# Where the adaLN columns and the context squares stand in the opening of a hybrid attention/GLA layer

## The chip, the cores and the metric

One NeuronCore of a Trainium2 chip runs the whole kernel. The metric is device time in microseconds of one execution, the median of several runs; lower is better.

## The reference, cut to what matters

One backbone layer over 256 latent tokens and 256 context tokens, width 2048. Both streams are normalized, scaled and shifted by columns that come from the conditioning vectors, and go through one wide projection. The change lies in this first part alone:

```python
mod_x = jnp.split((jax.nn.silu(c) @ w_mod[l] + b_mod[l])[:, None, :], 6, axis=-1)
mod_c = jnp.split((jax.nn.silu(c_ctx) @ w_mod[l] + b_mod[l])[None, None, :], 6, axis=-1)
# modulate(x, g, shift, scale) = rms_norm(x, g) * (1 + scale) + shift
... = proj(modulate(x, g_mix[l], mod_x[0], mod_x[1]))          # qa, ka, va, qb, kb, vb, ...
... = proj(modulate(ctx, g_mix[l], mod_c[0], mod_c[1]))
```

Windowed attention, gated linear attention, the merge and the convolutional feed-forward part follow; they are the same in both kernels.

## The kernel before

Activations lie transposed: channels on the 128 partitions, 256 tokens along the free axis, in 16 channel tiles ("kt") of 128. Every fp32 operand of a large product is split into a high part (ScalarE, `whi`, `h00hi`, line 207 or 495) and the rest (VectorE, `wlo`, `h00lo`, line 208 or 496), and three products are added up: high by high, high by low, low by high. In a tile's name h00lo the first digit is the stream (0 latent, 1 context), the second the half of the channels.

The scale and shift columns aren't there when the kernel starts. They are computed in five groups of channel tiles, `GROUPS` = (first tile, count) = (0,2), (2,2), (4,4), (8,4), (12,4), so that the projection can start on the first two tiles while the rest of the modulation matrix is still being loaded. For each group and each of the two parts (part 1 is the scale, part 0 the shift) `mod_both` makes steps: each step loads 1 MB of the matrix (`mraw`) and multiplies it by the conditioning vector (`pm`, line 95; 16 profile records of 256 columns for a step of the first two groups, 8 records of 512 columns for one of the others). After the last step VectorE transposes the result (`mtr`, line 324), and `end` turns it into columns: two small products on TensorE (`pcol`, line 95), four copies on VectorE (line 334) and an addition. `affine_scale` then multiplies the tokens by scale and by the row of 1/rms (`rrow`, lines 485 and 488), `affine_shift` adds the shift and splits (lines 495 and 496).

The row of 1/rms of the context comes from `square_sums(1)`: four squares on ScalarE (line 427, each 128x1024), additions on VectorE (lines 433 and 435), a sum over the channels on TensorE (`pr`, line 448), and the chain of `factor_row` (lines 457 to 462).

Order. Within the opening all TensorE instructions are chained in the order of the code (`pe_seq`), and all loads in theirs (`load`, queue of SyncE). On ScalarE and VectorE a scheduler sets the order, with single ties by `in_order(a, b)`. The projections used in the opening are columns QB (two blocks of 512), KB and VB of `w_in`. They accumulate in four PSUM banks (`acc`), which an evacuation has to free (line 503 into `qb0`, 556 and 572 into the tile kb0, 558 and 575 into vb0 for the first group, additions at line 505 for later ones).

The first group runs QB, QB+512, KB, VB for the latents, then KB, VB for the context. While the second group is multiplied, the steps of the third are called at six places, by `mid()`: before and inside QB+512, after QB+512, inside KB, after KB, inside VB. The list `steps` says how many steps each place takes. `end` of the third group was put off to the next `tick()` (the start of the next pair of channel tiles) by `defer(0, fn)`.

Of the kernel before, what the change touches and what calls it, by code (L numbers as in the profile page):

```python
# [11 lines left out]
AF = mybir.ActivationFunctionType  # L12
# [12 lines left out]
QA, KA, VA, QB, KB, VB, RB = 0, 2048, 2560, 3072, 4096, 5120, 7168  # L25
# [6 lines left out]
def layer_kernel(ctx, tc, A, out):  # L32
    nc = tc.nc
    V, S, G, PE = nc.vector, nc.scalar, nc.gpsimd, nc.tensor
# [12 lines left out]
    w_in = A["w_in"][0]  # L47
# [16 lines left out]
    def in_order(*ins):  # L64

        for a, b in zip(ins, ins[1:]):
            tc.add_manual_dep(b, a.name, mybir.DependencyInfo(
                mybir.DependencyClass.NoSync, mybir.DependencyReason.DATA), reason="order")
# [12 lines left out]
    def mm(*a, **k):  # L81

        r = pe_seq(PE.matmul(*a, **k))  # L83
        last[0] = r.ins
        return r
# [63 lines left out]
    def defer(n, fn):  # L149

        later.append([n, fn])
# [37 lines left out]
    def wload(src):  # L189
        n = src.shape[0] // P  # L190
        raw = wr.tile([P, 2, 512], F32, name="raw", tag="raw")
        load(raw[:, 0:n, :], src.rearrange("(c p) d -> p c d", p=P))
        return raw
# [65 lines left out]
    def proj_T(w, c0, kts, rhs, evac, mid=None):  # L259

        n = len(rhs)
        per = 2 // n
        banks = [acc.tile([P, 512], F32, name="acc", tag="acc") for _ in range(4 // per)]
        for k0 in kts[::2]:
            tick()
            nk = min(2, kts[-1] + 1 - k0)
            hi, lo = wsplit(w[k0 * P:(k0 + nk) * P, c0:c0 + 512])
            for part in range(2):
                if part:
                    (mid or midway)()  # L270
                for f in range(4):
                    for k in range(nk):
                        kt = k0 + k
                        w_ = (lo if part else hi)[:, k, f * P:(f + 1) * P]
                        for i, r in enumerate(rhs):
                            b = (f % per) if n == 1 else i
                            o = banks[f // per][:, b * T:(b + 1) * T]
                            ahi, alo = r(kt)
                            mm(o, w_, ahi, start=(kt == kts[0] and b == 0 and part == 0),
                                      stop=(kt == kts[-1] and part == 1), skip_group_check=True)  # L280
                            if part == 0:
                                mm(o, w_, alo, start=False, stop=False, skip_group_check=True)
        for i in range(len(banks)):
            evac(i, banks[i])
# [111 lines left out]
    def rms_scale(ss, n, shape):  # L396
# [13 lines left out]

    groups = GROUPS
    mods = [[mod_both(part, t0, n, dst, put) for part, dst in ((1, scale1), (0, shift1))]
            for (t0, n), put in zip(groups, [None, None] + 3 * [lambda fn: defer(0, fn)])]

    rrow1 = []
    kbt = M("kb0", [P, 4, 512])
# [2 lines left out]
    def square_sums(s):  # L419

        pr = bank("pr", (P, T), side=True)
        parts, whole = [], None
        for i in range(4):
            x_ = xr[2 * s + i // 2][:, (i % 2) * 4:(i % 2) * 4 + 4, :]
            q = wr.tile([P, 4, T], F32, name="sq", tag="raw")
            if s + i:
                S.activation(q, x_, AF.Square)
            else:
                V.tensor_tensor(q, x_, x_, op=ALU.mult)
                parts.extend(q[:, k, :] for k in range(4))  # L430
                continue
            h = q[:, 0:2, :]
            V.tensor_tensor(h, h, q[:, 2:4, :], op=ALU.add)
            if s and whole is not None:
                V.tensor_tensor(whole, whole, h, op=ALU.add)
            elif s:
                whole = h
            elif i == 2:
                V.tensor_tensor(h[:, 0, :], h[:, 0, :], h[:, 1, :], op=ALU.add)
                parts.append(h[:, 0, :])  # L440
            else:
                parts.extend(h[:, k, :] for k in range(2))
        if s:
            parts = [whole[:, 0, :], whole[:, 1, :]]

        def add_up(lo, hi):
            for i in range(lo, hi):
                pe_seq(PE.matmul(pr, ones[:, 0:P], parts[i], start=(i == 0), stop=(i == len(parts) - 1)))

        return pr, add_up  # L450
# [19 lines left out]
    def h_all(s):  # L470
        return lambda kt: (hh[s][kt // 8][:, kt % 8, :], hl[s][kt // 8][:, kt % 8, :])
# [11 lines left out]
    def affine_scale(s, t0, n):  # L483
        sc = scale1[:, s, t0:t0 + n]
        V.scalar_tensor_tensor(sc, sc, 1.0, gm1[:, t0:t0 + n], op0=ALU.add, op1=ALU.mult)
        for kt in range(t0, t0 + n):
            xk = xr[2 * s + kt // 8][:, kt % 8, :]
            V.scalar_tensor_tensor(xk, xk, scale1[:, s, kt:kt + 1], rrow1[s], op0=ALU.mult, op1=ALU.mult)

    def affine_shift(s, t0, n):  # L490
        for kt in range(t0, t0 + n):
            xk = xr[2 * s + kt // 8][:, kt % 8, :]
            sh = shift1[:, s, kt:kt + 1]
            hi, lo = hh[s][kt // 8][:, kt % 8, :], hl[s][kt // 8][:, kt % 8, :]
            j = S.activation(hi, xk, AF.Identity, bias=sh).ins
            i = V.scalar_tensor_tensor(lo, xk, sh, hi.bitcast(F32), op0=ALU.add, op1=ALU.subtract).ins
        return i, j


    def add_to(dst, first):  # L500
        def evac(i, b):
            if first:
                S.activation(dst(i), b, AF.Copy)
            else:
                V.tensor_tensor(dst(i), dst(i), b, op=ALU.add)
        return evac
# [35 lines left out]
    qb0 = [W2("fc", "qb0", [P, 512]) for _ in range(4)]  # L542
    kts = ALL[0:2]
# [3 lines left out]
    i, j = affine_shift(0, *groups[0])  # L547
    hold.append(i)
    hold_hi.extend([None, j])
    proj_T(w_in, QB, kts, [h_all(0)], add_to(lambda i: qb0[i], True))  # L550
    proj_T(w_in, QB + 512, kts, [h_all(0)], add_to(lambda i: qb0[2 + i], True))
    wk, wv = wsplit_raw(raws[0]), wsplit_raw(raws[1])
    early.extend([wk, wv])
    half = lambda i, o: kbt[:, 2 * i:2 * i + 2, o:o + T]
# [8 lines left out]
    a1()  # L563
    affine_scale(1, *groups[0])
    affine_shift(1, *groups[0])
    ea()
    b0()
    b1()
    for s in range(2):
        affine_scale(s, *groups[1])  # L570
    early.extend([wk, wv])
    proj_T(w_in, KB, kts, [h_all(1)], lambda i, b: S.activation(half(i, T), pair_of(b), AF.Copy), mid=eb)
    i0, j0 = affine_shift(0, *groups[1])
    proj_nat(w_in, 0, VB, kts, [h_tok(1, 0), h_tok(1, 1)],
             lambda i, b: S.activation(vb0[:, 2 + i, :], b, AF.Copy))
    early.extend(wload(w_in[2 * P:4 * P, c:c + 512]) for c in (QB, QB + 512, KB, VB))
    hold.append(i0)
    hold_hi.append(j0)
    i, j = affine_shift(1, *groups[1])
# [3 lines left out]
    for gi, (t0, n) in enumerate(groups):  # L583
        if gi == 0:
            continue
        kts = ALL[t0:t0 + n]
        flush()
        while bg_steps:
            bg_steps.pop(0)()
        flush()  # L590
        mid = None
        if gi + 1 < len(groups):
            bg_steps.extend(mods[gi + 1][0] + mods[gi + 1][1])
            ticks = 4 * ((n + 1) // 2)
            bg_rate[:] = [1.4 * len(bg_steps) / ticks + 0.01, 0.0]
            if gi == 1:
                bg_rate[:] = [0.0, 0.0]
                steps = iter([1, 2, 1, 2, 2, 0])

                def mid():  # L600
                    pin[0] = last[0]
                    for _ in range(next(steps)):
                        bg_steps.pop(0)()
                    pin[0] = None
        if t0 == 8:
            more_h(1)
        for s in range(2):
            if gi > 1:
                affine_scale(s, t0, n)
                affine_shift(s, t0, n)  # L610
            if s == 0:
                for j in range(2):
                    if j and mid is not None:
                        mid()
                    proj_T(w_in, QB + j * 512, kts, [h_all(0)], add_to(lambda i, j=j: qb0[2 * j + i], False),
                           mid=mid if j else None)
                if mid is not None:
                    mid()
        proj_T(w_in, KB, kts, [h_all(0), h_all(1)], add_to(lambda i: kbt[:, i, :], False), mid=mid)
        if mid is not None:  # L620
            mid()
        proj_nat(w_in, 0, VB, kts, h_xc, add_to(lambda i: vb0[:, i, :], False), mid=mid)
        if gi > 2:
            opening.clear()
# [421 lines left out]
    for j in range(4):  # L1046
# [6 lines left out]
        def at_evac(t, b, a1=a1, j=j):  # L1053
            if j == 0:
# [5 lines left out]
                 lambda t, b, a2=a2: sig.append(S.activation(a2[t], b, AF.Sigmoid)))  # L1060
# [79 lines left out]
    for t in range(2):  # L1140
        v_, r_, q_, c_ = (fac[:, t, i:i + 1] for i in range(4))
        x_ = ss1[:, t, 3:4]
# [31 lines left out]
    for half, blocks in enumerate((range(0, 6), range(6, 11))):  # L1174
        n = len(blocks)
# [128 lines left out]
```

## Time and profile before

| | us |
|---|---|
| median of 3 runs | 1984.97 (1984.95 to 1985.31) |
| the profiled execution | 1985.05 |
| its span, first to last instruction | 1983.1 |

The profile is of one execution. A row of the timeline gives the start, the duration, the engine, the line, the operation with output and inputs, the count, and in brackets the engine's idle time before it with what ended it. TensorE (PE) is busy for 99% of the span, VectorE (DVE) for 71%, ScalarE (ACT) for 49%. PEld is the loading of weights. An instruction with q behind the engine's name (SPq) is one that issues a load and keeps no engine busy.

### The profile page before, as it was taken

What the parts mean: (1) busy time and instruction counts of PE and PEld (TensorE: products, weight loads), DVE (VectorE), ACT (ScalarE), POOL (GpSimd) and SP (SyncE); (2) the same over time, 40 slices, a digit from 0 to 9 for tenths busy, and PEclk for the clock granted to TensorE, in tenths of its full rate; (3) what the DMA queues carried; (4) which work ended last, traced back from release to release, by engine and by line L of the source; (5) the groups of instructions that cost most, each with busy time, mean ns of one, the idle gap of its engine ahead of it and who ended that gap; (6) DMA issues with size and microseconds to landing.
All of it is one profiled execution on the core that took longest, in us unless ns stands there. A gap on an engine that the chain in (4) does not pass through costs nothing.

```text
span 1983.1 us, 27131 instructions
## 1 busy us (share of the span) xinstructions
PE 1958.6 (99%) x10324; PEld 1637.9 (83%) x10324; DVE 1400.0 (71%) x2150; ACT 971.2 (49%) x1413; POOL 44.5 (2%) x61
## 2 busy tenths in 40 slices
PE   7999999999999999999999999999999999999999
PEld 5679888888887788888888888888888888888887
DVE  5765667876858888777776457889887555677754
ACT  4323555553345666444444445755555334555532
POOL 0010010112000000000000000000000000000000
PEclk9999999999999999999999999999999999999999
DMA  9965222336753456888888668688886566666563
GB/s 379 413 262 178 65 85 75 107 98 196 249 156 112 127 181 210 267 289 287 295 281 272 232 224 282 193 271 278 259 275 232 192 193 190 190 190 184 190 215 113
DMA packets 183603, 420.90 MB, mean 212 GB/s; under 512 B 12544, under 2 KB 12768, under 8 KB 178736
## 3 DMA queue, kind: packets, MB, share of 16 engines
q1 hardware_dynamic: 181856, 413.19, 63.8%
q0 software_dynamic: 1440, 5.80, 1.0%
q8 instruction: 81, 1.33, 0.3%
q14 instruction: 50, 0.41, 0.1%
q10 hardware_dynamic: 176, 0.17, 0.0%
HBM read 416.98 MB, written 2.13 MB: 211 GB/s over the span
## 4 chain that ended last, share of the span: by engine, by line
PE 68%; DVE 0%; ACT 0%; issue 0%; DVEq 0%
PE acc L83 52%; PE accs L83 12%; PE poa L95 1%; PE pS L95 1%; PE ptp L98 1%; PE pto L98 0%; PE ptx L98 0%; DVE wlo L208 0%; ACT s L973 0%; PE ptq L98 0%; DVE s L978 0%; DVE yd L1225 0%; DVE yd L1219 0%; DVE raw L365 0%; ACT whi L207 0%
## 5 line engine op out<-in xcount | busy, mean ns | idle before, releaser
L208 DVE TENSOR_TENSOR wlo<-raw,whi 128x1024 fp32r<-128x1024 f32 x568 | 694.8, 1225 | 435.0 <-ACT whi L207 394.7
L207 ACT ACTIVATE whi<-raw 128x1024 fp32r<-128x1024 f32 x568 | 601.1, 1059 | 773.3 <-PE acc L83 619.4
L83 PE MATMUL accs<-h,whi 128*128 128x512 f32 x704 | 176.3, 392 | 0.0
L83 PE MATMUL acc<-h,whi 128*128 128x512 f32 x640 | 160.4, 392 | 0.0
L83 PEld LDWEIGHTS accs<-h,whi 128*128 128x128 f32 x704 | 126.6, 189 | 22.6
L83 PE MATMUL acc<-whi,h01hi 128*128 128x512 f32 x352 | 139.9, 398 | 0.0
L83 PE MATMUL acc<-whi,h00hi 128*128 128x512 f32 x352 | 139.0, 395 | 0.0
L83 PE MATMUL acc<-whi,h00lo 128*128 128x512 f32 x352 | 138.0, 392 | 0.0
L83 PE MATMUL acc<-whi,h01lo 128*128 128x512 f32 x352 | 137.9, 392 | 0.0
L83 PE MATMUL acc<-whi,al 128*128 128x512 f32 x352 | 137.0, 389 | 0.0
L83 PE MATMUL acc<-whi,ah 128*128 128x512 f32 x352 | 137.0, 389 | 0.0
L83 PEld LDWEIGHTS acc<-h,whi 128*128 128x128 f32 x640 | 115.1, 189 | 20.6
L83 PEld LDWEIGHTS accs<-h,wlo 128*128 128x128 f32 x704 | 96.0, 190 | 6.8
L83 PE MATMUL acc<-wlo,h01hi 128*128 128x512 f32 x352 | 98.7, 396 | 0.0
L83 PE MATMUL accs<-h,wlo 128*128 128x256 f32 x704 | 98.2, 282 | 0.0
L83 PE MATMUL acc<-wlo,h00hi 128*128 128x512 f32 x352 | 97.7, 394 | 0.0
L83 PE MATMUL acc<-wlo,ah 128*128 128x512 f32 x352 | 94.3, 389 | 0.0
L83 PEld LDWEIGHTS acc<-h,wlo 128*128 128x128 f32 x640 | 87.4, 190 | 6.3
L83 PE MATMUL acc<-h,wlo 128*128 128x256 f32 x640 | 89.4, 282 | 0.0
L365 DVE CUSTOM_DVE_ANT_0 raw<-raw,csrow,pack 128x1024 f32<-128x1024 f32 x64 | 81.7, 1284 | 0.0
L83 PEld LDWEIGHTS acc<-whi,ah 128*128 128x128 f32 x352 | 66.1, 188 | 13.7
L83 PEld LDWEIGHTS acc<-whi,al 128*128 128x128 f32 x352 | 66.1, 188 | 13.6
(389 smaller groups left out, 3566.0 us busy)
## 6 DMA issues: line engine op xcount, KB each, us to landing
raw<-in_w_in SPq DMA_DIRECT2D x208, 512.0 KB, 4.4
raw<-in_w_up SPq DMA_DIRECT2D x176, 512.0 KB, 3.9
raw<-in_w_modT SPq DMA_DIRECT2D x128, 512.0 KB, 4.6
raw<-in_w_down SPq DMA_DIRECT2D x88, 512.0 KB, 3.7
mraw<-in_w_mod SPq DMA_DIRECT2D x32, 1024.0 KB, 13.3
raw<-in_w_attn_o SPq DMA_DIRECT2D x32, 512.0 KB, 4.9
raw<-in_w_gla_o SPq DMA_DIRECT2D x32, 512.0 KB, 4.7
raw<-in_w_out SPq DMA_DIRECT2D x32, 512.0 KB, 4.8
```

The costliest lines, as they stand in the source:

```text
L83: r = pe_seq(PE.matmul(*a, **k))
L95: return pe_seq(after(PE.matmul(*a, **k)))
L98: return pe_seq(after(PE.transpose(*a)))
L207: j = S.activation(hi[:, 0:n, :], raw[:, 0:n, :], AF.Copy).ins
L208: i = V.tensor_tensor(lo[:, 0:n, :], raw[:, 0:n, :], hi[:, 0:n, :].bitcast(F32), op=ALU.subtract).ins
L365: i0 = V.tensor_tensor_reduce(out=raws[i], in0=raws[i], in1=row[0], scale=1.0, scalar=d if h else bmod[:, b0:b0 + 1], op0=ALU.mult, op1=AL ...
```

## The change

Four places of the opening move; no operation is added or taken away.

- The two evacuations after each QB block of the first group are kept in a list, and the first and third context squares are tied behind the second and fourth of them on ScalarE.
- For the second group, `end` of the scale (`ea`) is called behind both steps of the shift, not between the two parts. `affine_scale` of its context tiles is called after VB of the context.
- `end` of the third group goes to a list `pend`, and each `mid()` first calls what stands there. The places take 1, 2, 1, 4, 0, 0 steps where they took 1, 2, 1, 2, 2, 0.
- `affine_scale` of the third group is called inside KB of the second, and the latent `affine_shift` inside VB. Both stood ahead of the third group's first projection.

```diff
-            for (t0, n), put in zip(groups, [None, None] + 3 * [lambda fn: defer(0, fn)])]
+            for (t0, n), put in zip(groups, [None, None] + [lambda fn: pend.append(fn)] + 2 * [lambda fn: defer(0, fn)])]
+    pend = []
...
             if s + i:
-                S.activation(q, x_, AF.Square)
+                j = S.activation(q, x_, AF.Square).ins
+                if s and i in (0, 2):
+                    in_order(evicted[i + 1], j)
...
-    proj_T(w_in, QB, kts, [h_all(0)], add_to(lambda i: qb0[i], True))
-    proj_T(w_in, QB + 512, kts, [h_all(0)], add_to(lambda i: qb0[2 + i], True))
+    evicted = []
+    for j in range(2):
+        proj_T(w_in, QB + j * 512, kts, [h_all(0)],
+               lambda i, b, j=j: evicted.append(S.activation(qb0[2 * j + i], b, AF.Copy).ins))
...
-    ea()
     b0()
     b1()
-    for s in range(2):
-        affine_scale(s, *groups[1])
+    ea()
+    affine_scale(0, *groups[1])
...
+    affine_scale(1, *groups[1])
     early.extend(wload(w_in[2 * P:4 * P, c:c + 512]) for c in (QB, QB + 512, KB, VB))
...
-                steps = iter([1, 2, 1, 2, 2, 0])
+                steps = iter([1, 2, 1, 4, 0, 0])
+
+                def next_columns():
+                    if pend:
+                        pend.pop(0)()
+
+                def scale_2():
+                    next_columns()
+                    for s in range(2):
+                        affine_scale(s, *groups[2])
+
+                also = iter([next_columns] * 3 + [scale_2, next_columns, lambda: affine_shift(0, *groups[2])])
 
                 def mid():
                     pin[0] = last[0]
+                    next(also)()
                     for _ in range(next(steps)):
                         bg_steps.pop(0)()
                     pin[0] = None
...
-            if gi > 1:
+            if gi > 2:
                 affine_scale(s, t0, n)
+            if gi > 2 or (gi == 2 and s):
                 affine_shift(s, t0, n)
```

What the program makes of it, at three places. First ScalarE during the first group's products; qb_241 to qb_244 are the four evacuations of QB and QB+512, xr_87 and xr_88 hold the context tokens. Before:

```order
L207 ACTIVATE whi<-raw 128x1024 x2
L427 ACTIVATE sq<-xr_87 128x1024 x2
L207 ACTIVATE whi<-raw 128x1024
L503 ACTIVATE qb_241<-acc 128x512
L503 ACTIVATE qb_242<-acc 128x512
L427 ACTIVATE sq<-xr_88 128x1024 x2
L503 ACTIVATE qb_243<-acc 128x512
```

ScalarE there now:

```order
L207 ACTIVATE whi<-raw 128x1024 x3
L556 ACTIVATE qb_241<-acc 128x512
L556 ACTIVATE qb_242<-acc 128x512
L428 ACTIVATE sq<-xr_87 128x1024 x2
L556 ACTIVATE qb_243<-acc 128x512
L556 ACTIVATE qb_244<-acc 128x512
L428 ACTIVATE sq<-xr_88 128x1024 x2
```

Each pair of squares moved behind a pair of evacuations, and the third split of weights moved ahead of them.

Second, VectorE from the context's sum of squares to the context tokens; scale_104 are the scale columns, here those of the second group. Before:

```order
L457 TENSOR_SCALAR vrow<-pr 128x256
L324 STREAM_TRANSPOSE mtr<-pm_2_389 128x256
L460 TENSOR_TENSOR vrow<-rrow 128x256
L334 COPY scale_104<-pcol_2_429 32x2x2
L461 TENSOR_TENSOR vrow<-vrow 128x256
L334 COPY scale_104<-pcol_2_429 32x2x2
L462 SCALAR_TENSOR_TENSOR rrow<-vrow,rrow 128x256
L334 COPY scale_104<-pcol_2_429 32x2x2
L488 SCALAR_TENSOR_TENSOR xr_87<-xr_87,scale_104,rrow 128x256 x2
```

VectorE there now:

```order
L460 TENSOR_SCALAR vrow<-pr 128x256
L324 STREAM_TRANSPOSE mtr<-pm_2_389 128x256
L463 TENSOR_TENSOR vrow<-rrow 128x256
L464 TENSOR_TENSOR vrow<-vrow 128x256
L465 SCALAR_TENSOR_TENSOR rrow<-vrow,rrow 128x256
L491 SCALAR_TENSOR_TENSOR xr_87<-xr_87,scale_104,rrow 128x256 x2
```

The copies of the second group's columns no longer stand between the steps of the context's row.

Third, TensorE around KB of the second group; pm_4_ and pcol_4_ belong to the third group. Before, the scale columns stood ahead of KB's first half, the shift columns right behind the last steps, ahead of VB (acc<-whi,h00hi):

```order
L95 MATMUL pm_4_564<-mraw,cS 32x512 x4
L95 MATMUL pcol_4_627<-mtr,pack 32x32
L83 MATMUL acc<-h00hi,whi 128x256
...
L83 MATMUL acc<-h10hi,wlo 128x256
L95 MATMUL pm_4_670<-mraw,cS 32x512 x8
L95 MATMUL pcol_4_721<-mtr,pack 32x32
L83 MATMUL acc<-whi,h00hi 128x512
```

TensorE there now:

```order
L83 MATMUL acc<-h10lo,whi 128x256
L95 MATMUL pcol_4_663<-mtr,pack 32x32
L95 MATMUL pm_4_680<-mraw,cS 32x512 x16
L83 MATMUL acc<-h00hi,wlo 128x256
...
L83 MATMUL acc<-h10hi,wlo 128x256
L95 MATMUL pcol_4_727<-mtr,pack 32x32
L83 MATMUL acc<-whi,h00hi 128x512
```

All four shift steps now stand in the middle of KB (x16 are 32 records of the profile), and each pair of column products has products of KB between it and the steps that it needs. The queue of loads on SyncE has the same order as before, and behind the third group's columns the order on every engine is the same.

## The prediction

> **What bounds the kernel now.** I read the page first, then TensorE's waits, then the opening's rows engine by engine, then the loads. The first line of the page:
>
> ```profile
> PE 1958.6 (99%) x10324; PEld 1637.9 (83%) x10324; DVE 1400.0 (71%) x2150; ACT 971.2 (49%) x1413; POOL 44.5 (2%) x61
> ```
>
> TensorE sets the time, so the change can only win what TensorE waits for where the order was changed. The waits of TensorE from 30 to 165 us (who waits, for whom: total, times, longest):
>
> ```profile
> PE pcol L95 <- DVE mtr L324: 2.6, 4, 0.8
> PE acc L83 <- DVE wlo L208: 1.1, 3, 0.6
> PE acc L83 <- ACT h10hi L495: 0.7, 1, 0.7
> PE acc L83 <- ACT qb L503: 0.4, 1, 0.4
> PE acc L83 <- DVE h10lo L496: 0.2, 1, 0.2
> ```
>
> That is 5.0 us in all. The 1.1 us for `wlo` fall on later groups, whose order stays. What is within reach is 2.6 + 0.7 + 0.4 + 0.2 = 3.9 us, 0.2% of the time. The loads of this stretch, by windows (length, busy time of PE, PEld, DVE, ACT and POOL with counts, then TensorE's granted clock, the loads' share of the DMA engines, GB/s):
>
> ```profile
> 28.00:66.00 38.00, 34.96 (x286) 26.80 (x285) 27.29 (x62) 18.15 (x29) 0.00 (x0) 1.00 1.02 416
> 66.00:116.00 50.00, 48.92 (x358) 36.38 (x357) 32.80 (x67) 13.98 (x21) 0.00 (x0) 1.00 0.99 394
> 116.00:128.00 12.00, 12.00 (x72) 8.73 (x70) 4.75 (x6) 4.91 (x8) 0.00 (x0) 1.00 0.00 0
> ```
>
> Until about 112 us the DMA engines are never free (share 1.02, 0.99). So a load in this stretch can't land earlier, however early TensorE asks: the queue's order is the same and the bytes ahead of it are the same. From 116 to 128 us nothing is loaded: there the loads wait for TensorE, and shift with it. The landing times up to about 112 us are thus fixed points against which TensorE's earlier arrival has to be held.
>
> TensorE's rows at the places in question:
>
> ```profile
> 32.05 0.39 PE L83 MATMUL acc<-h00hi,whi 128*128 128x256 f32 x1 [0.40 <-ACT qb L503]
> 37.87 1.07 PE L95 MATMUL pm<-mraw,cS 128*32 128x256 f32 x16
> 38.87 1.13 PE L448 MATMUL pr<-sq,ones 128*128 128x256 f32 x4
> 41.57 0.20 PE L95 MATMUL pcol<-mtr,pack 128*32 128x16 f32 x1 [0.57 <-DVE mtr L324]
> 44.27 0.38 PE L83 MATMUL acc<-h10hi,whi 128*128 128x256 f32 x1 [0.72 <-ACT h10hi L495]
> 47.43 0.24 PE L95 MATMUL pcol<-mtr,pack 128*32 128x16 f32 x2 [0.33 <-DVE mtr L324]
> 60.47 1.06 PE L95 MATMUL pm<-mraw,cS 128*32 128x512 f32 x8
> 62.37 0.25 PE L95 MATMUL pcol<-mtr,pack 128*32 128x32 f32 x2 [0.84 <-DVE mtr L324]
> 62.55 0.39 PE L83 MATMUL acc<-h00hi,whi 128*128 128x256 f32 x1
> 66.56 1.92 PE L95 MATMUL pm<-mraw,cS 128*32 128x512 f32 x16
> 70.52 1.92 PE L95 MATMUL pm<-mraw,cS 128*32 128x512 f32 x16
> 73.28 0.25 PE L95 MATMUL pcol<-mtr,pack 128*32 128x32 f32 x2 [0.84 <-DVE mtr L324]
> 73.46 0.50 PE L83 MATMUL acc<-whi,h00hi 128*128 128x512 f32 x1
> ```
>
> Each `pcol` stands right behind the steps whose transposed result it needs; 73.46 is the first product of VB of the second group, the point at which I compare the two kernels.
>
> **The change part by part.**
>
> *Context squares behind the evacuations.* The last products of QB, then ScalarE and VectorE before:
>
> ```profile
> 27.65 1.12 PE L83 MATMUL acc<-h00hi,wlo 128*128 128x256 f32 x8
> 28.23 1.06 ACT L427 ACTIVATE sq<-xr 128x1024 f32<-128x1024 f32 x1 [0.90 <-DMA xr<-in_ctxT]
> 30.48 1.04 ACT L207 ACTIVATE whi<-raw 128x1024 fp32r<-128x1024 f32 x1
> 31.42 1.07 ACT L503 ACTIVATE qb<-acc 128x512 f32<-128x512 f32 x2
> 32.38 2.00 ACT L427 ACTIVATE sq<-xr 128x1024 f32<-128x1024 f32 x2
> 35.52 0.69 DVE L435 TENSOR_TENSOR sq<-sq 128x512 f32<-128x512 f32 x1
> ```
>
> The evacuations ran at 31.42, behind two squares and a split, and TensorE waited 0.40 us for the bank. Now they run as soon as QB is done (27.65 + 1.12 = 28.8), near 29 us, so the 0.40 goes. The price: the squares move behind them. First pair from about 30.0 to 32.1, second pair behind the other two evacuations (1.07 again) to about 35.2; the last square ended at 34.38 before, so the sums are ready near 36.9 where they were ready at 35.52 + 0.69 = 36.2. `pr` asks for them at 38.87 - 0.4 = 38.5. The cover is 1.6 us. Gain 0.4; bounds 0 and 0.4.
>
> *Second group's columns behind both parts.* Without the old `pcol` at 41.57 TensorE goes on into the shift's two steps, and the four copies leave the chain of the context's row on VectorE:
>
> ```profile
> 41.44 0.38 DVE L460 TENSOR_TENSOR vrow<-rrow 128x256 f32<-128x256 f32 x1
> 42.54 0.43 DVE L462 SCALAR_TENSOR_TENSOR rrow<-vrow,rrow 128x256 f32<-128x256 f32 x1
> 43.19 0.88 DVE L488 SCALAR_TENSOR_TENSOR xr<-xr,scale,rrow 128x256 f32<-128x256 f32 x2
> ```
>
> From 41.44 to 43.19 is 1.75 us; three operations of 0.43 are 1.3; about 0.4 of copies goes. With the 0.4 from above the first context product stands at 44.27 - 0.8 = 43.5. Two other things must be there by then. One is the shift's second step, whose load is one of these fixed points:
>
> ```profile
> L104 SPq DMA_DIRECT2D mraw<-in_w_mod x1: 328/328/328, 26.9 to 26.9; - x1
> DMA to landing us min/median/max: 15.0/15.0/15.0
> ```
>
> It lands at 26.9 + 15.0 = 41.9, a step of this kind takes 38.87 - 37.87 = 1.0, and `pcol` some 0.2: 43.1, just ahead. So of the 0.57 wait at 41.57 nothing comes on top; it only becomes part of the same 0.8. The `pcol` at 47.43 now finds `mtr` done during the products: 0.33 more. Sum up to here 1.1 us. The latent second-group tokens are scaled and shifted in time only if VectorE keeps up; I give this bounds of 0.5 and 1.4, and show below that the end hardly depends on it.
>
> *Third group's columns amid the products.* Two things change on TensorE. First, behind the one step at 60.47 comes KB at once. A step of this size costs 1.0 until the next product, two cost 1.85:
>
> ```profile
> 79.14 1.07 PE L95 MATMUL pm<-mraw,cS 128*32 128x512 f32 x8
> 80.14 0.39 PE L83 MATMUL acc<-h00hi,whi 128*128 128x256 f32 x1
> 87.27 1.92 PE L95 MATMUL pm<-mraw,cS 128*32 128x512 f32 x16
> 89.12 0.39 PE L83 MATMUL acc<-h00hi,whi 128*128 128x256 f32 x1
> ```
>
> KB began at 62.55 and would begin at 60.47 + 1.0 = 61.47: 1.0 gained when I leave 0.1 for the two `pcol` products in their new place. Second, the last `pcol` has KB's second half between it and the steps. Before, from 66.56 to VB: 73.46 - 66.56 = 6.90. Now four steps, 1.85 + 2 x 0.85 = 3.55; KB's second half as before, from the end of the first two steps (66.56 + 1.85 = 68.41) to 70.52, 2.1; `pcol` 73.46 - 73.28 = 0.2; together 5.85. So 1.05 more. Free of loads the sum would be 1.1 + 1.0 + 1.05 = 3.15 us.
>
> But the fourth of these steps used to start at 70.52 + 0.85 = 71.4, and now wants to start at 66.56 - 1.1 - 1.0 + 3 x 0.85 = 67.0. Its load:
>
> ```profile
> L104 SPq DMA_DIRECT2D mraw<-in_w_mod x1: 328/328/328, 58.6 to 58.6; - x1
> DMA to landing us min/median/max: 8.9/8.9/8.9
> ```
>
> It lands at 58.6 + 8.9 = 67.5. TensorE must wait about 0.5 us there, a new wait that the change itself makes. From it: 67.5 + 1.0 (the step) + 2.1 (KB's second half) + 0.2 (`pcol`) = 70.8 for the first product of VB, against 73.46: **2.65 us gained**, whatever was won earlier, as long as that is over 0.6 of the 1.1. What was won beyond that is spent waiting.
>
> *What moves on the other engines.* The scaling of the third group (VectorE, eight operations) goes from before `kb`'s additions to before them still, 1.0 to 2.0 us earlier with TensorE. The shift of its latent tokens moves ahead of TensorE's need, from the start of the third group into VB of the second: no wait of TensorE stood there, so I cost it at nothing; its cover is VB itself (73.46 to 79.14, 5.7 us). The queue of loads keeps its order, so no load is moved past another.
>
> *Behind it.* Later waits (1.1 us for `wlo`) stand in an unchanged order and shift along, and so do the loads from 128 us on, which wait for TensorE. Nothing I see takes the 2.65 back.
>
> [...] The row says 416 GB/s from 28 to 66 us. [...]
>
> **The rivals.**
>
> *A, no new wait:* the load lands half a microsecond earlier, for instance because loads ahead of it are issued a little sooner. Against it speaks the share of 1.02. It gives the sum free of loads, 3.15: 1985.05 - 3.15 = 1981.9; with every wait in reach gone, 3.9, 1981.15.
>
> *B, part is given back:* the first two parts give less than 0.6, since the squares come late or the second group's shift waits on VectorE, or VB waits for its banks: the four additions that free them now run close to its start. Each is a wait of 0.5 to 1.5 us. It gives a gain of 1 to 2, 1983.0 to 1984.0.
>
> *C, it does nothing:* the time won in the opening comes back in a later wait for a load. For it: until 112 us loads are short. Against it: in the windows TensorE is busy for 48.92 of 50.00 us from 66 to 116, and no row there waits for a load. 1985.
>
> *D, slower:* the fourth shift step's load becomes the bound. All four steps now stand ahead of KB's second half, so each microsecond by which this load lands behind 67.5 holds up KB's second half and VB. It breaks even at 67.5 + 2.65 = 70.15. If it came later by a tenth of the 38 us for which the queue has run full by then, 71.3, the kernel would be slower by 1.2: 1986.2; over 0.2% slower from 74.1 on. For it: the queue is full and the same rate isn't promised. Against it: TensorE frees the buffers for these loads earlier, not later. [...]
>
> **How the numbers follow.** The profiled execution took 1985.05 us (span 1983.1, 1.95 around it), 0.08 above the median of the runs shown. 1985.05 - 2.65 = 1982.4; set against the median, 1982.3. Chances: the forecast 0.66, A 0.13, B 0.12, C 0.04, D 0.05. The range from A's inner end to B's outer end, 1981.3 to 1984.2, leaves out C, D and the far end of A. A measurement of this kernel can tell about 0.2%, 4 us, from no change. The forecast, A, B, C and the near part of D all lie within that: 3.9 is the most that TensorE waits for in the stretch. Faster by over 0.2% needs more than all of that, 0.06; slower by over 0.2% needs D by 6.6 us against the forecast, or a stall that I don't see, 0.06; within, 0.88.
>
> **What would show it.** In the profile after: no wait at the first KB product of the first group (32.05); the evacuations near 29 and the squares near 30 on ScalarE; the first context product near 43.5; no wait of `pcol` at 47, 62 and 73; a new wait of `pm` for `mraw` of about half a microsecond near 67; VB's first product near 70.8; and from there every row 2.6 us earlier, the span near 1980.5. Wrong would be: VB's first product still behind 72; a wait of more than 1 us at that load; or new waits between 71 and 112 us.

## The result, and the profile after

| | median us | lowest to highest | runs |
|---|---|---|---|
| before | 1985.34 | 1984.64 to 1987.11 | 22 |
| changed | 1982.39 | 1982.08 to 1983.02 | 22 |

The ratio is 0.9983 (0.9978 to 0.9989), and the medians are 2.95 us apart: within the 0.2% that the prediction takes as no change, though the interval lies clear of 1. The forecast was 1982.3. Before's times fall into two groups 1.7 us apart (14 runs at 1984.6 to 1985.8, 8 at 1986.6 to 1987.1); the changed kernel has one group of 1 us. The profiled executions have spans of 1983.1 and 1980.7 us.

The first line of the page after, and TensorE's waits from 30 to 165 us:

```profile
PE 1956.6 (99%) x10324; PEld 1637.2 (83%) x10324; DVE 1400.1 (71%) x2150; ACT 971.8 (49%) x1413; POOL 45.6 (2%) x61
```

```profile
PE pm L95 <- DMA mraw<-in_w_mod: 2.3, 2, 1.5
PE acc L83 <- DVE wlo L208: 1.1, 3, 0.6
```

All four waits that the change was aimed at (3.9 us) are gone. In their place stand 2.3 us for loads of modulation weights, and not where I expected them. TensorE's rows after:

```profile
39.80 1.07 PE L95 MATMUL pm<-mraw,cS 128*32 128x256 f32 x16 [0.81 <-DMA mraw<-in_w_mod]
42.38 1.81 PE L95 MATMUL pm<-mraw,cS 128*32 128x256 f32 x16 [1.51 <-DMA mraw<-in_w_mod]
44.16 0.58 PE L83 MATMUL acc<-h10hi,whi 128*128 128x256 f32 x1
61.10 0.39 PE L83 MATMUL acc<-h00hi,whi 128*128 128x256 f32 x1
65.12 0.22 PE L95 MATMUL pcol<-mtr,pack 128*32 128x32 f32 x1
65.20 3.60 PE L95 MATMUL pm<-mraw,cS 128*32 128x512 f32 x29
71.11 0.47 PE L83 MATMUL acc<-whi,h00hi 128*128 128x512 f32 x1
```

The waits stand at 39.80 and 42.38, ahead of the context products; the four steps from 65.20 run through without one. VB's first product is at 71.11 (73.46 before): 2.35 us earlier, and the span is shorter by 2.4. Nothing behind this point takes it back. ScalarE did what the change says (the forecast was near 29 and near 30):

```profile
28.26 1.06 ACT L556 ACTIVATE qb<-acc 128x512 f32<-128x512 f32 x2
29.21 2.01 ACT L428 ACTIVATE sq<-xr 128x1024 f32<-128x1024 f32 x2
```

The windows of the changed kernel, three stretches (fields as in those of before):

```profile
28.00:66.00 38.00, 35.69 (x286) 26.94 (x288) 23.63 (x52) 17.32 (x29) 0.00 (x0) 0.96 1.02 416
66.00:116.00 50.00, 49.73 (x359) 37.88 (x352) 35.00 (x76) 16.49 (x26) 0.00 (x0) 1.00 0.99 394
```

The loads move at the same 416 and 394 GB/s. The granted clock from 28 to 66 us is 0.96 where it was 1.00. Shorter windows of the same execution place the loss:

```profile
40.00:44.00 4.00, 2.49 (x33) 1.08 (x26) 2.48 (x6) 0.91 (x2) 0.00 (x0) 0.82 1.03 384
44.00:48.00 4.00, 4.00 (x30) 3.80 (x26) 2.80 (x14) 0.00 (x0) 0.00 (x0) 0.75 1.05 413
```

A share of 0.82 and one of 0.75 of two windows of 4 us are 0.72 + 1.00 = 1.72 us of full clock lost. From 44 to 46 us the share is 0.50, so the loss stands for some 3.4 us at half clock, called a half-clock stretch below. Before's execution had such a stretch too, but at another place:

```profile
20.00:24.00 4.00, 3.58 (x25) 1.98 (x26) 0.79 (x4) 1.06 (x1) 0.00 (x0) 0.57 1.05 390
```

(0.43 x 4 = 1.72 us again.) So the two profiles shown do not differ by the change alone. That became the main question of the experiments, beside the one on the new bound: is it the load that lands at 67.5?

### The profile page after: what moved, and what is told of

Its sections match the earlier page's. It is cut to its first block, busy times and chain, and to the rows that moved or that the text cites. A ratio compares the mean times of both kernels' runs of the same rounds, so it can differ in the third digit from the quotient of the medians.

```text
span 1980.7 us, 27130 instructions
## 1 busy us (share of the span) xinstructions
PE 1956.6 (99%) x10324; PEld 1637.2 (83%) x10324; DVE 1400.1 (71%) x2150; ACT 971.8 (49%) x1413; POOL 45.6 (2%) x61
## 3 DMA queue, kind: packets, MB, share of 16 engines
q8 instruction: 81, 1.33, 0.3%
## 4 chain that ended last, share of the span: by engine, by line
PE 68%; DVE 0%; ACT 0%; issue 0%; DVEq 0%
PE acc L83 52%; PE accs L83 12%; PE poa L95 1%; PE pS L95 1%; PE ptp L98 1%; PE pto L98 0%; PE ptx L98 0%; DVE wlo L208 0%; ACT s L991 0%; PE ptq L98 0%; DVE s L996 0%; DVE yd L1243 0%; DVE yd L1237 0%; DVE raw L365 0%; ACT whi L207 0%
```

## The experiments

Each kernel but the last was timed in 11 runs, one of them profiled, beside before on the same chip. "VB" below is VB's first product of the second group (73.46 in the profile before).

**The kernel before, again.** No edit.

> The kernel before, unchanged. Theory 1 (hidden waits): nothing to see, about 1985.3 us. Theory 2 (clock stretch): the 22 times of before fall into two groups, 1984.6 to 1985.8 and 1986.6 to 1987.1, because a stretch of 3.4 us at half the granted clock lies in different places from run to run; this kernel should show the same two groups, and its profile the half-clock stretch either at 20 to 24 us, as before, or among the products behind 37 us if this run is one of the slower group.

1985.22 (ratio 0.9999, 0.9990 to 1.0008), VB at 73.81. This execution has no half-clock stretch (mean granted clock 1.000). TensorE's first product of the first group and of KB, `pr` and VB, then ScalarE:

```profile
23.84 0.38 PE L83 MATMUL acc<-h00hi,whi 128*128 128x256 f32 x1 [0.46 <-ACT h00hi L495]
32.39 0.39 PE L83 MATMUL acc<-h00hi,whi 128*128 128x256 f32 x1 [1.98 <-ACT qb L503]
39.22 1.13 PE L448 MATMUL pr<-sq,ones 128*128 128x256 f32 x4
73.81 0.50 PE L83 MATMUL acc<-whi,h00hi 128*128 128x512 f32 x1
```

```profile
28.57 1.06 ACT L427 ACTIVATE sq<-xr 128x1024 f32<-128x1024 f32 x1 [2.47 <-DMA xr<-in_ctxT]
29.85 1.06 ACT L427 ACTIVATE sq<-xr 128x1024 f32<-128x1024 f32 x1 [0.22 <-DMA xr<-in_ctxT]
31.76 1.07 ACT L503 ACTIVATE qb<-acc 128x512 f32<-128x512 f32 x2
```

Here the bank wait is 1.98 us, not 0.40. The evacuations stand in ScalarE's order behind two squares, and those wait for the context's loads (2.47 and 0.22 us in the rows above). TensorE went on at 32.39 here and at 32.05 in the profile that I predicted from, though QB had begun later there, by the half-clock stretch:

```profile
25.08 0.38 PE L83 MATMUL acc<-h00hi,whi 128*128 128x256 f32 x1 [0.29 <-ACT h00hi L495]
```

That is 25.08 instead of 23.84, and 1.24 of the wait lay hidden behind it.

**The squares' part alone.**

```diff
-                S.activation(q, x_, AF.Square)
+                j = S.activation(q, x_, AF.Square).ins
+                if s and i in (0, 2):
+                    in_order(evicted[i + 1], j)
...
```

The rest of this edit keeps the evacuations in `evicted`, as the changed kernel does.

> Only the tie of the context squares behind the evacuations. Theory 1: the 0.4 us wait for the bank at 32 us goes, the products behind it come 0.4 us earlier, and since the load of the shift's second step (41.9) then binds, at most 0.4 us arrive at the end: 1984.9 against 1985.3. Theory 2: the clock stretch decides, the two groups of times stay, and the median moves by less than the distance of the groups (1.6 us) in either direction.

1982.96 (0.9988, 0.9979 to 0.9997), VB at 71.47. Its rows, again without a half-clock stretch (mean granted clock 1.000):

```profile
36.88 1.13 PE L450 MATMUL pr<-sq,ones 128*128 128x256 f32 x4
42.22 1.07 PE L95 MATMUL pm<-mraw,cS 128*32 128x256 f32 x16 [1.52 <-DMA mraw<-in_w_mod]
58.48 1.06 PE L95 MATMUL pm<-mraw,cS 128*32 128x512 f32 x8
71.47 0.50 PE L83 MATMUL acc<-whi,h00hi 128*128 128x512 f32 x1
```

`pr` came at 39.22 in the execution of before without a stretch: 2.34 us from this part, where I had costed 0.4. At the first context product 1.4 of it is left (43.22 against 44.62), behind the new wait for the load. The rest comes back right after: in before two of these products took 0.47 us, at the pace of the context's tokens, and here 0.24. VB keeps 2.34.

**The second group's part alone.**

```diff
-    ea()
     b0()
     b1()
-    for s in range(2):
-        affine_scale(s, *groups[1])
+    ea()
+    affine_scale(0, *groups[1])
...
+    affine_scale(1, *groups[1])
```

> Only the second group's columns behind both parts. Theory 1: the waits of pcol at 41 and 47 us go (0.57 and 0.33), but the shift's second step now waits for its load, which lands near 42; 0.3 to 0.8 us gained at the first product of QB of the second group, 1984.5 to 1985.0. Theory 2: the new wait for the load invites a half-clock stretch behind it, among the context products, which costs up to 1.3 us there: no gain or a small loss in such runs.

1985.68 (0.9998, 0.9989 to 1.0006): no difference that can be measured. The profiled execution shows where a half-clock stretch hurts; the product behind the bank wait, and the window that it opens:

```profile
32.36 0.39 PE L83 MATMUL acc<-h00hi,whi 128*128 128x256 f32 x1 [1.99 <-ACT qb L503]
```

```profile
32.00:36.00 4.00, 3.64 (x18) 3.64 (x19) 3.84 (x6) 3.66 (x6) 0.00 (x0) 0.60 1.02 424
```

The bank wait of 1.99 us is followed by a granted clock of 0.60 from 32 to 36 us, amid products, and VB comes at 74.34.

**The third group's part alone.**

```diff
-                steps = iter([1, 2, 1, 2, 2, 0])
+                steps = iter([1, 2, 1, 4, 0, 0])
...
+                    next(also)()
...
```

> Only the third group's columns amid the products. Theory 1: both waits of pcol at 62 and 73 us go, 2.0 us gained at VB's first product, without a wait at the fourth step's load, since nothing is won ahead of it: 1983.3 against 1985.3. This is most of the whole change. Theory 2: the opening up to 60 us is that of before, so the two groups of times should stay, 1.6 us apart, each 2.0 us lower; if the spread of this kernel is as small as that of the whole change (1982.1 to 1983.0), theory 2 is wrong on what made the groups.

1983.25 (0.9991, 0.9982 to 1.0000), VB at 71.86; no column wait is left at 62 and 73, and the bank wait is 1.65 at 32.41. For these three kernels the times lie in two groups each, as those of before do. Lower group against lower group (before 1985.31 there), the parts give 2.4, 1.0 and 2.2 us: 5.6 in all. The whole change gives 2.7 to 2.9 so counted. Something caps it.

**The changed kernel, again.** No edit.

> The changed kernel as it is. Theory 1 (the load of the fourth shift step of the third group, landing at 67.5 us, caps what the opening can win): in an execution without a half-clock stretch among the products the fourth step waits 1.0 to 1.5 us for that load and VB's first product stands at 70.8; in one with a stretch, as the first profile of the changed kernel had at 42.6 us, the stretch takes the place of that wait. All times lie within 1 us, near 1982.4. Theory 2 (the load of the second group's second shift step at 42.3 us caps): TensorE waits there 1.5 us, and no load is waited for at 67 us.

1982.07 (0.9983, 0.9974 to 0.9992). This execution had its half-clock stretch where the profile before had it, 0.57 from 20 to 24 us, so the two can be held row against row:

```profile
38.16 1.13 PE L451 MATMUL pr<-sq,ones 128*128 128x256 f32 x4
42.02 1.07 PE L95 MATMUL pm<-mraw,cS 128*32 128x256 f32 x16 [0.87 <-DMA mraw<-in_w_mod]
43.14 0.38 PE L83 MATMUL acc<-h10hi,whi 128*128 128x256 f32 x1
59.83 0.39 PE L83 MATMUL acc<-h00hi,whi 128*128 128x256 f32 x1
63.94 2.74 PE L95 MATMUL pm<-mraw,cS 128*32 128x512 f32 x21
67.46 1.06 PE L95 MATMUL pm<-mraw,cS 128*32 128x512 f32 x8 [0.78 <-DMA mraw<-in_w_mod]
70.56 0.25 PE L95 MATMUL pcol<-mtr,pack 128*32 128x32 f32 x2
70.74 0.50 PE L83 MATMUL acc<-whi,h00hi 128*128 128x512 f32 x1
```

The fourth step starts at 67.46 behind a wait of 0.78 us for its load, and VB at 70.74: the forecast was 67.5, 0.5 and 70.8. Against the first profile after, KB is 1.27 us earlier (59.83, 61.10), VB only 0.37 (70.74, 71.11). The wait at 67.46 took up most of the difference. The load that this step waits for:

```profile
L104 SPq DMA_DIRECT2D mraw<-in_w_mod x1: 328/328/328, 57.0 to 57.0; - x1
DMA to landing us min/median/max: 10.5/10.5/10.5
```

It is issued at 57.0 and lands at 67.5. In before it was issued at 58.6 and landed at 67.5 too, in the first profile after at 58.2 and 67.5. In all 14 profiled executions it was issued between 56.6 and 60.6 and landed between 67.4 and 67.6: asked for earlier, it doesn't land earlier.

**The changed kernel without the second group's part.**

```diff
+    ea()
     b0()
     b1()
-    ea()
-    affine_scale(0, *groups[1])
+    for s in range(2):
+        affine_scale(s, *groups[1])
...
-    affine_scale(1, *groups[1])
```

> The changed kernel with the second group's columns put back as they were before: the squares and the third group alone. If the load at 67.5 us caps the opening (theory 1), the second part is worth nothing on top of the other two: within 0.5 us of the changed kernel, 1982.1 to 1982.9, with a shorter wait at 67.5. If the parts add up (rival), it is slower than the changed kernel by what the second part won alone, 0.9 us: 1983.1.

1982.29 (0.9984, 0.9975 to 0.9993): as the whole change. The steps and VB:

```profile
64.97 3.70 PE L95 MATMUL pm<-mraw,cS 128*32 128x512 f32 x29
70.89 0.50 PE L83 MATMUL acc<-whi,h00hi 128*128 128x512 f32 x1
```

Without this part TensorE comes about a microsecond later to the steps (64.97 where it was 63.94), finds the load there without a marked wait, and is at VB 0.15 us later. Both executions have the early stretch (0.57 from 20 to 24 us in each); in them, what the second part wins is spent at the load.

**The fourth step behind KB instead of in its middle**, the shift columns then in VB.

```diff
-                steps = iter([1, 2, 1, 4, 0, 0])
+                steps = iter([1, 2, 1, 3, 1, 0])
...
+                def shift_2():
+                    next_columns()
+                    affine_shift(0, *groups[2])
...
```

> The changed kernel with 1, 2, 1, 3, 1, 0 steps, its shift columns of the third group in VB, the rest unchanged. Theory 1: without the cap at 67.5 the executions without a half-clock stretch gain 1.3 us, 1981.1, those with one nothing, so the times fall into two groups again. Theory 2: 1982.4, as the changed kernel.

1982.01 (0.9983, 0.9974 to 0.9992), no better than the changed kernel on the same chip (1982.07). Its rows, and then the one of the changed kernel's second execution that answers to the last:

```profile
58.53 1.06 PE L95 MATMUL pm<-mraw,cS 128*32 128x512 f32 x8
69.41 0.50 PE L83 MATMUL acc<-whi,h00hi 128*128 128x512 f32 x1
76.75 0.38 PE L83 MATMUL acc<-h00hi,whi 128*128 128x256 f32 x1 [0.19 <-ACT h00hi L498]
80.38 1.06 PE L95 MATMUL pm<-mraw,cS 128*32 128x512 f32 x8
```

```profile
80.47 1.07 PE L95 MATMUL pm<-mraw,cS 128*32 128x512 f32 x8
```

With the load out of the way VB is at 69.41, 1.33 us earlier. Of these 0.78 are the wait for the load, 0.3 come of an execution without the early stretch (a granted clock of 1.00 from 20 to 24 us; the steps start at 63.63, not 63.94), and some 0.2 are the column products that now stand behind VB's start. So the load did hold VB up, by about 0.8 us here. At 80.4 only 0.1 of it is left, because the columns now stand in VB and are late for the third group's first product (76.75), and the products behind it start with gaps.

The row at 58.53 shows something else. It is the step ahead of KB, and with the squares' part alone it stood at 58.48. Neither execution has a half-clock stretch (mean granted clock 1.000 in both), and this kernel has the second group's part as well, yet it comes no earlier: both waited for the same load at 42 us (1.52 us there, 1.55 here), which landed at 42.1 and 42.3. So without the early stretch the second part's gain ends already at that load, and the cap at 67.5 isn't the only one.

**The fourth step halfway through KB's second half**, the columns at the end of KB as in the changed kernel.

```diff
+                    if part and f == 2 and late is not None:
+                        late()
...
-                steps = iter([1, 2, 1, 4, 0, 0])
+                steps = iter([1, 2, 1, 3, 1, 0, 0])
...
```

> The changed kernel with the fourth shift step of the third group called halfway through KB's second half, the three others where they were. Theory 1: half of KB's second half (1 us) covers the wait for the load, the other half the transpose; 0.6 to 1.0 us less than the changed kernel, 1981.2, VB's first product near 69.9. If instead the columns' chain behind the step binds (as in the version with the step behind KB), pcol waits for mtr and nothing is won: 1982.1.

1981.89 (0.9981, 0.9972 to 0.9990), in two groups: seven runs at 1981.35 to 1981.94, four at 1982.94 to 1983.88. The profiled execution is of the later four, with half clock from 42 us on (0.75 from 40 to 44 us, 0.83 from 44 to 48):

```profile
68.75 1.06 PE L95 MATMUL pm<-mraw,cS 128*32 128x512 f32 x8
71.37 0.25 PE L95 MATMUL pcol<-mtr,pack 128*32 128x32 f32 x2 [0.41 <-DVE mtr L326]
71.55 0.50 PE L83 MATMUL acc<-whi,h00hi 128*128 128x512 f32 x1
```

No wait for the load, and 0.41 us for the transpose instead. Seven runs are below every run of the changed kernel but its lowest (1981.93), but the spread that the changed kernel lost is back. Against the two medians of the changed kernel it gains 0.2 and 0.5 us; the intervals overlap, and it stays open whether this version is better.

**The second group's last shift step amid the context's KB**, so that the load at 42 us isn't waited for.

```diff
-    b1()
-    ea()
-    affine_scale(0, *groups[1])
+
+    def part_0():
+        b1()
+        ea()
+        affine_scale(0, *groups[1])
...
-    proj_T(w_in, KB, kts, [h_all(1)], lambda i, b: S.activation(half(i, T), pair_of(b), AF.Copy), mid=eb)
+    proj_T(w_in, KB, kts, [h_all(1)], lambda i, b: S.activation(half(i, T), pair_of(b), AF.Copy), mid=part_0)
+    eb()
```

> The changed kernel with the second group's last shift step moved from ahead of the context's products into the middle of the context's KB, its columns behind KB. Theory 1: the 1.5 us wait at 42 us goes, and all of it is waited for at 67.5 us instead; no gain in most executions, 1982.4. Theory 2: 1 to 1.5 us less, 1981.1.

1983.64 (0.9991, 0.9981 to 1.0000): the median is 1.6 us above that of the changed kernel. The runs fall into two groups, five at 1982.4 to 1982.9 and six at 1983.6 to 1984.2, and the profiled execution is of the lower one (1982.40, VB at 71.06, 0.3 us behind the changed kernel). The wait for the load at 42 is gone; in its place 1.06 us for `h10hi` stand at 41.89, and another new wait stands later. TensorE, then ScalarE:

```profile
50.90 0.39 PE L83 MATMUL acc<-h00hi,whi 128*128 128x256 f32 x1 [0.93 <-ACT whi L207]
```

```profile
48.99 0.91 ACT L498 ACTIVATE h00hi<-xr,shift 128x256 fp32r<-128x256 f32 x2 [1.55 <-DVE shift L337]
49.81 1.99 ACT L207 ACTIVATE whi<-raw 128x1024 fp32r<-128x1024 f32 x2
```

The shift columns come later, ScalarE waits 1.55 us for them, and the split of the next weights is queued behind. All six runs of the upper group have a mean granted clock of 0.999, against 1.000 in the profiled execution; where their half-clock stretch lies stays open, since none of them was profiled. **Both of these edits together** (this one and the fourth step behind KB):

> As f1, and the fourth shift step of the third group moved behind KB (1, 2, 1, 3, 1, 0 steps), its columns into VB. Theory 1: the load at 67.5 no longer holds up KB's second half, so the opening's gains come through: 2.0 to 2.5 us less than the changed kernel, 1980.2, with executions with a half-clock stretch up to 1.7 us above. Theory 2: the split adds nothing to f1, 1981.1. A loss would come from the shift's columns, now in VB, if the third group's first product waits for them.

1985.06 (1.0000, 0.9991 to 1.0008): a miss. The same wait for `whi` stands at 52.40 (0.93 us), half clock lies across 42 to 46 us (mean granted clock 0.999), and VB is at 72.43. Against the profiled execution of the first edit alone VB is 1.37 us later and the whole time 2.66 (1985.06, 1982.40), so some 1.3 more are lost behind VB's start, about what the split alone lost there.

**Before, with 24 idle transposes in front of KB of the first group**, to fill the bank wait.

```diff
+    fill = bank("fill")
+    for _ in range(24):
+        pe_seq(PE.transpose(fill[:, 0:P], ident, ident))
```

> The kernel before with 24 idle transposes on TensorE ahead of KB of the first group, where it waits up to 2.0 us for the bank. Theory 2 (that wait, seen by the clock's control, brings the half-clock stretch at 33 us in part of the runs): the slower group near 1986.7 goes, the times stay near 1985.2, up to 1 us more in runs in which the wait is short. If the two groups have another cause: both stay, 1.6 us apart.

1986.77 (1.0004, 0.9995 to 1.0013), in two groups of five and six runs. The profiled execution had its stretch early; a window and the fill:

```profile
20.00:24.00 4.00, 3.59 (x25) 1.99 (x26) 0.78 (x4) 1.06 (x1) 0.00 (x0) 0.57 1.05 388
```

```profile
31.50 2.78 PE L558 MATMUL fill<-pack 128*128 128x128 f32 x24
```

With the early stretch there was little wait left to fill, and the fill itself pushed KB back. The two groups are 1.2 us apart, as far as the early stretch delays QB (25.09 here, 23.84 without it), so they may come of that stretch alone; no run of the lower group was profiled. The test doesn't separate the explanations. **A third profile of before**, in the hope of one of its later runs:

> The kernel before, one more look. If it falls into the slower group (about one run in three), theory 2 expects a half-clock stretch behind the wait for the bank, at 32 to 36 us; if into the faster, either no stretch or one at 20 to 24 us.

One run, 1985.17, with a stretch from 20.5 to 24 us (mean granted clock 0.999), a bank wait of 0.63 and VB at 73.60: not one of them.

## Why the prediction held, point by point

*The end, set by the load at 67.5.* Right, and shown from both sides: the wait appears where it was worked out and about as long (0.78 at 67.46 against 0.5 at 67.5); a part less leaves VB where it was (70.89); the step moved out of the way brings VB to 69.41. In the first profile after the wait is missing, because the stretch at 42.6 brought TensorE to the fourth step at 67.73, just behind the landing (67.5); that VB stood near the forecast there too (71.11) is partly luck. VB moved by 2.72 us in the executions that can be held against each other (forecast 2.65), spans of 1980.2 and 1980.7 (forecast near 1980.5). The landing itself stayed put (67.4 to 67.6 in every profiled execution), so rival D found no ground, and rival A was wrong in its one condition. Two remarks on the numbers. The forecast was set against a median of three runs, none of them of before's upper group; against the lower group's median (1985.07) the gain is 2.7, against all runs 2.95. And the range 1981.3 to 1984.2 is wider than the ends that the prediction names for it, 1981.9 and 1984.0, without a reason given.

*Squares behind evacuations.* The term that was mis-sized. I gave 0.4, with 0.4 as its upper bound. Row against row with the early stretch it is 38.87 - 38.16 = 0.7; without the stretch 39.22 - 36.88 = 2.34. I took the wait from one execution, and in that one a late QB hid most of it. The row that could have warned me stood in the prediction: the square that waited 0.90 us for the context's load. The evacuations queued behind that load let TensorE go on at 32.05 and, in the second execution, at 32.39; the wait was that time less TensorE's arrival, 31.65 and 30.41.

*Second group's columns.* The first context product was forecast at 43.5 and came at 43.14 (44.16 under half clock). But its reason was wrong: I had the load of the last shift step landing "just ahead", at 41.9, and took it as no wait; it is waited for by 0.87 to 1.5 us, and the context tokens are no longer what comes last. This landing takes the second part's whole gain where there is no early stretch (58.48 and 58.53 above). The 0.33 at 47.43 went as said.

*Third group's columns.* From the first step to VB 5.85 us were worked out free of loads; 71.11 - 65.12 = 6.0 were measured. KB's second half kept its 2.1 (68.46 to 70.56). TensorE reached the steps 2.7 us earlier instead of 2.1, and the cap made that the same.

*Rival C* was partly true without deciding: of what the opening gained, 0.9 to 2.3 us turned into waits for loads at 40 to 42. The total held because the cap at 67.5 lies behind both errors: a larger gain ahead of it only lengthened the wait there (none at the steps from 64.97, 0.78 us at those from 63.94), as the prediction said of its second sum. That is also why a total that is right to 0.1 us says little about its terms.

*A gain not forecast:* the upper group of before's times is gone. What I can show is that a 3.4 us stretch where products run costs 1.3 us more at KB than the early one (61.10 against 59.83) and that the wait at 67.46 takes up most of it (0.37 are left at VB, 71.11 against 70.74). The mean granted clock that is on record for each run says more. One stretch loses 1.72 of 1983 us, so a run without one has a mean of 1.000 and a run with one 0.999; the 14 profiled executions agree with this, each of them. Of the 93 runs of before beside the experiments all 28 of the upper group have 0.999, and the other 65 are divided: 26 have 1.000, 39 have 0.999. So each run of the upper group has a stretch, but a stretch alone doesn't put a run there. In the second 11 runs of the changed kernel five have 1.000 and six 0.999, and all lie within 0.3 us.

That the stretch of before's later runs lies behind the bank wait, as in the experiment on the second group, fits the numbers, but no such run of before was profiled; its place remains argued.

## What to carry to other kernels

A wait in one profile is a difference of two times: look at which of them is fixed (a landing, or work queued behind one) and which moves with the engine, and take a second execution before sizing it. Where loads never pause, as here up to about 112 us (DMA share 1.02 from 28 to 66 us, 1.03 from 66 to 108), find the landing that lies last ahead of the end and work the end out from it; gains ahead of it don't add (5.6 us of parts became 2.9, and the landing at 42 had taken its share before the one at 67.5). And whoever lifts such a cap should first look for the chain that is next: here the columns, the shift and the split behind it took back 1.2 of 1.3 us.

## What the runs showed of the hardware

TensorE's granted clock fell to half for a stretch of some 3.4 us in 9 of 14 profiled executions (mean granted clock 0.999 in these, 1.000 in the other 5), near a wait of 1.4 to 2 us of TensorE, and not always at the same place in two executions of one kernel: from about 20 us (0.57 from 20 to 24), from 33 (0.60 from 32 to 36), from 42.6 (0.82 and 0.75 from 40 to 48), or not at all. The share was 0.50 in the 2 us from 44 to 46, which lie wholly inside that last stretch. In the first profile of each kernel the stretch took 1.72 us of full clock. A wait alone doesn't bring it: all 14 executions have one of 1.4 us that ends between 20.3 and 20.8 us, and 5 of them have no stretch anywhere. What decides where a stretch falls stays open.
